# A hybrid decoder block on one core: the input stage reordered, two sums of x as adding DMAs, rotation tables later

## The chip, the core and the metric

The kernel runs on one core of a Trainium2 chip. The metric is device time in microseconds (us) of one execution; lower is better. All times of the trace are microseconds from the start of the profiled span.

## The reference

One layer, 1024 tokens of width 1024, float32:

```python
h = rms_norm(x, mix_norm_g)
z_a, q, k, v, gate_logits = split(h @ w_in)                  # w_in: 1024 x 5888
y_a = chunked_spatial_gating(gelu(z_a), ...)                 # chunks of 128 tokens, 4 channel groups
y_b = dilated_mixture_attention(rope(q), rope(k), v)         # 3 groups of 4 heads of 64
merged = sigmoid(g_a) * (y_a @ w_branch_a) + sigmoid(g_b) * (y_b @ w_branch_b)
x = x + merged @ w_out
h2 = rms_norm(x, ffn_norm_g)
a, val = split(h2 @ w_up)                                    # 2 x 2816 columns
x = x + (gelu(causal_dwconv3(a)) * val) @ w_down
return rms_norm(x, final_norm_g)
```

The rotation `rope` turns the first 16 of 64 dimensions of each head by angles `position * inv_freq`. The change lies wholly in how `h @ w_in` begins.

## The kernel before

**Products in parts.** Every large product is made of float32 operands that are split in two: `hi`, rounded to the matmul's float32r format by ScalarE, and `lo`, the rest, a subtraction on VectorE. Three passes (hi x hi, hi x lo, lo x hi) give the product. A 128x512 operand thus costs one ScalarE and one VectorE instruction, and a product over half the width (QK = 4 tiles of 128) twelve matmuls of 128x512.

**The input product.** Its columns go in pairs of 2 x 128 columns (`PAIRS`): three pairs `zv`, then three pairs each for the attention groups, then gates and `zu`. x stands in `X` transposed (channels on the partitions): 8 rows `kt` of 1024 tokens. `quarter(i, j, kt)` is its block of tokens half `i` and channel half `j`: A11, A12 (i = 0), A21, A22 (i = 1).
- Pairs 0 and 1 are plain products (`plain_step`, `plain_final`): for pair n, token half h and column half i, 24 matmuls over all 8 rows, on parts of the *raw* x times the gain (`raw_left`). The norm's factor per token is applied later, when V is written out of PSUM (`turn_v`).
- From pair 2 (`FIRST`) on, each pair takes seven products P1 to P7 instead of eight (Strassen's scheme in Winograd's form). Their left operands (`LEFT`) are parts of the *scaled* x: A11, A12, A22 and the sums S1 = A21 + A22, S2 = S1 - A11, S3 = A11 - A21, S4 = A12 - S2; the right ones are columns of w_in and sums of them (`weight_op`). P2 goes on in P1's PSUM bank, P4 in P7's and P3 in P5's (`SHARED`), after ScalarE or VectorE has read the first product out of it.

**The norm.** ScalarE squares the rows of x (`square_row`, tokens on the partitions, loaded by `load_rows`), POOL takes the root (`root`), VectorE makes four diagonals of it (`diagonal`), and TensorE multiplies them by ones (`spread`), which gives the factor of each token along the free axis. With it VectorE scales `X` in place (`scale_x`). All that happens for each token half h.

**The rotation tables.** `rot_tables` gives a chain of small VectorE steps (`some(n)` does the next n), two sines on ScalarE, sixteen widening copies on ScalarE (`wide`) and four turns (`turns`: four transposes on TensorE and a copy back on ScalarE each), whose result is in `YC` and is first needed by the rotation of pair 3.

**Order.** `beginning()` writes the order of VectorE, ScalarE and TensorE by hand up to pair 2's first product; then a loop over `in_order` does one product per step `i` (`in_product`), with `in_ahead` preparing operators ahead and `meanwhile(i)` the left operands that are missing. Up to `ORDERED` = 6, the end of pair 2, ScalarE and VectorE keep the written order; later a scheduler orders them. Loads are issued by SP in the order written. At step 3 the pool of `X` is closed: the tile V lies on its memory, and the copies of turned pairs into V (`turn_v`, two small PSUM banks, `ps_tr`) wait until the last part of x has been read.

In `beginning()` before, the plain products come in the order (pair, token half) = (0,0), (1,0), (0,1), (1,1); A11, A12 and A22 are split during them; the sums S1 and S2 are made on VectorE, S3 and S4 on POOL; the turns stand between the last plain products. `meanwhile` splits S3 after P1, S1 after P2 and S4 after P7.

Of the kernel before, what the change touches and what calls it, by code (L numbers as in the profile page):

```python
# [16 lines left out]
ALU = mybir.AluOpType  # L17
# [76 lines left out]
def block_kernel(  # L94
# [60 lines left out]
    def f32(ap):  # L155
        return ap.bitcast(F32)
# [189 lines left out]
    in_load(0, 1)  # L346
    in_load(1, 0)
    load_rows(0)
    in_load(1, 1)
    load_x(1, range(KT))  # L350
# [27 lines left out]
    def diagonal(h):  # L378
        for b in range(4):
            dg = dgs[h][:, b * P : (b + 1) * P]  # L380
            nc.vector.tensor_scalar(dg, ident, rss[h][:, b : b + 1], None, ALU.mult)
# [10 lines left out]

    def in_left(name, kt, src):

        arena, row = IN_ROWS[name]
        t = left[name, kt] = two(arena, row + kt)
        return (
            lambda: nc.scalar.activation(t[:, 0], src, AF.Copy),
            lambda: nc.vector.tensor_tensor(t[:, 1], src, f32(t[:, 0]), ALU.subtract),
        )  # L400
# [16 lines left out]
    def parts_of(name, i, j):  # L417
        staggered((lambda: None, *in_left(name, kt, quarter(i, j, kt))) for kt in range(QK))

    U_ROWS = {(0, 0): (R, 0), (0, 1): (R, 8), (1, 0): (G1, 0), (1, 1): (R, 12)}
# [18 lines left out]
    def x_sum(n, kt):  # L441
        a11, a12, a21, a22 = (quarter(i, j, kt) for i in range(2) for j in range(2))
        if n == 1:
            nc.vector.tensor_tensor(a22, a21, a22, ALU.add)
        elif n == 2:
            nc.vector.tensor_tensor(a11, a22, a11, ALU.subtract)
        elif n == 3:
            nc.gpsimd.tensor_tensor(a21, a11, a21, ALU.subtract)
        else:
            nc.gpsimd.tensor_tensor(a12, a12, a11, ALU.subtract)  # L450
# [573 lines left out]
    def beginning():  # L1024

        chain, wide, turns = rot_tables(
            nc, lent, [[C[2][:, i, lower], C[2][:, i, upper]] for i in range(2)],
            acc_tile, ident, positions, YC,
# [18 lines left out]
        def product(n, h, i, k):  # L1047
            for kt in range(QK):
                plain_step(n, h, i, k, kt)
# [3 lines left out]
        for k in range(2):  # L1053
            weight(0, k, 0)
            for kt in range(k * QK, (k + 1) * QK):
                raw_parts(0, kt)
            product(0, 0, 0, k)
# [3 lines left out]
        some(4)  # L1061
        weight(1, 0, 0)
        weight(1, 1, 0)
        plain_final(0, 0, 0)
        for k in range(2):
            product(0, 0, 1, k)
        some(10)
# [4 lines left out]
        plain_final(0, 0, 1)  # L1072
        diagonal(0)
        for k in range(2):
            product(1, 0, 0, k)
        bc0 = spread(0)
        weight(1, 0, 1)
        weight(1, 1, 1)
        for kt in range(KT):
            raw_parts(1, kt)  # L1080
            scale_x(0, kt, bc0)
            some(1)
        plain_final(1, 0, 0)
        for b in range(4):
            square_row(1, b)
        root(1)
        for k in range(2):
            product(1, 0, 1, k)
        some(99)
        plain_final(1, 0, 1)  # L1090
        diagonal(1)
        product(0, 1, 0, 0)
        bc1 = spread(1)
        parts_of("A11", 0, 0)
        product(0, 1, 0, 1)
        parts_of("A12", 0, 1)
        for fn in wide:
            fn()
        for kt in range(KT):
            scale_x(1, kt, bc1)  # L1100
        plain_final(0, 1, 0)
        for k in range(2):
            product(0, 1, 1, k)
        plain_final(0, 1, 1)
        parts_of("A22", 1, 1)
        for kt in range(QK):
            x_sum(1, kt)
            x_sum(3, kt)
        in_ahead(0, 9, 2)
        turns[0]()  # L1110
        for k in range(2):
            product(1, 1, 0, k)
        turns[1]()
        plain_final(1, 1, 0)
        turns[2]()
        for k in range(2):
            product(1, 1, 1, k)
        turns[3]()
        plain_final(1, 1, 1)
        staggered(  # L1120
            (lambda kt=kt: x_sum(2, kt), *in_left("S2", kt, quarter(0, 0, kt)))
            for kt in range(QK)
        )
        for kt in range(QK):
            x_sum(4, kt)
# [21 lines left out]
    beginning()  # L1147
# [1137 lines left out]
```

## Time and profile before

| | |
|---|---|
| median of 3 runs | 1397.3 us (1396.05 to 1397.56) |
| the profiled execution's own time | 1395.51 us |
| its span | 1393.3 us |
| TensorE matmuls busy | 1367.7 us, 98% of the span, 6434 instructions |
| VectorE, ScalarE, POOL busy | 74%, 47%, 22% of the span |
| mean granted TensorE clock | 0.994 |

The profile has a page and views that answer from the same trace. In a row of the timeline stand start, duration, engine, line of the kernel, operation, output and inputs, and the count of merged instructions; in brackets the idle time before it and what ended it. Rows of waits give waiter, releaser, total time, count and longest. PE is TensorE, PEld its weight loads, DVE VectorE, ACT ScalarE, POOL GpSimd, SP the engine that issues most DMAs.

### The profile page before, as it was taken

To read this page: it belongs to the slowest core of one execution; us is meant where nothing else is said; L and a number is where in the kernel's file an instruction comes from. 1 tells how busy PE (TensorE), PEld (TensorE's weight loads), DVE (VectorE), ACT (ScalarE), POOL (GpSimd) and SP (SyncE) were. 2 spreads that over 40 slices of the span, in tenths; PEclk is the share of its full clock that TensorE was granted. 3 is DMA by queue.
4 is the path that set the end of the run, shared out by engine and by line. 5 is a ranking of instruction groups with operands and counts; after the bars stand their busy time and mean duration, and the time that the engine had idled before them with its cause. 6 is when DMAs were issued, how large, how long until landed. Compare 5 with 4: busy or idle time off the path is not lost.

```text
span 1393.3 us, 19245 instructions
## 1 busy us (share of the span) xinstructions
PE 1367.7 (98%) x6434; PEld 1133.6 (81%) x6434; DVE 1036.0 (74%) x1884; ACT 653.7 (47%) x1285; POOL 306.7 (22%) x299
## 2 busy tenths in 40 slices
PE   9789999999999999999999999999999999999997
PEld 7667888888888888888888878888888888888886
DVE  7878677676876987867789887766766667685674
ACT  8473255555553432534546444433333335455453
POOL 1302000000232000030001046555566553000002
PEclk9999999999999999999999999999999999999999
DMA  9014635364435997594743133333333327996563
GB/s 362 18 50 123 180 97 181 96 178 129 139 111 168 330 318 271 187 310 168 266 137 119 39 113 106 106 106 104 104 105 119 121 83 245 385 317 229 196 207 121
DMA packets 142787, 234.91 MB, mean 169 GB/s; under 512 B 13664, under 2 KB 57440, under 8 KB 142688
## 3 DMA queue, kind: packets, MB, share of 16 engines
q1 hardware_dynamic: 141248, 231.53, 49.7%
q10 hardware_dynamic: 1440, 2.16, 0.4%
q8 instruction: 51, 0.84, 0.3%
q14 instruction: 48, 0.39, 0.1%
HBM read 167.77 MB, written 64.29 MB: 167 GB/s over the span
## 4 chain that ended last, share of the span: by engine, by line
PE 83%; DVE 6%; DMA 5%; issue 3%; ACT 1%; POOL 1%; POOLq 0%; DVEq 0%; SPq 0%; ACTq 0%
PE in_P L486 25%; PE uP L1762 19%; PE dn L2020 10%; PE up L1762 8%; PE pa L1234 5%; PE wo_P L1595 4%; PE pu L827 2%; DMA dS<-gS 2%; PE pu L1741 2%; PE pb L1234 2%; PE pl L547 1%; PE pp L811 1%; DMA X<-in_xt_dram 1%; PE sc L772 1%; PE sc L773 1%
## 5 line engine op out<-in xcount | busy, mean ns | idle before, releaser
L486 PE MATMUL in_P<-R,G 128*128 128x512 f32 x1008 | 247.4, 398 | 6.1 <-ACT C L506 4.4
L486 PEld LDWEIGHTS in_P<-R,G 128*128 128x128 f32 x1008 | 187.5, 190 | 44.5 <-ACT C L506 4.8
L2020 PE MATMUL dn<-R 128*128 128x512 f32 x924 | 209.6, 389 | 0.0
L2020 PEld LDWEIGHTS dn<-R 128*128 128x128 f32 x924 | 173.4, 188 | 36.0
L165 ACT ACTIVATE G<-wr 128x512 fp32r<-128x512 f32 x126 | 79.1, 629 | 152.0 <-PE in_P L486 111.6
L165 ACT ACTIVATE R<-up 128x512 fp32r<-128x512 f32 x130 | 78.7, 627 | 123.7 <-DVE up L278 40.9
L1762 PE MATMUL up<-G,R 128*128 128x512 f32 x504 | 121.5, 391 | 1.5 <-DVE R L166 1.5
L486 PE MATMUL in_P<-G,G 128*128 128x512 f32 x504 | 122.8, 393 | 0.2 <-DVE C L513 0.2
L1762 PE MATMUL uP<-G,R 128*128 128x512 f32 x504 | 121.2, 389 | 0.0
L1762 PE MATMUL uP<-R 128*128 128x512 f32 x504 | 121.1, 389 | 0.0
L1762 PEld LDWEIGHTS up<-G,R 128*128 128x128 f32 x504 | 94.5, 188 | 22.5 <-DVE R L166 2.0
L1762 PEld LDWEIGHTS uP<-G,R 128*128 128x128 f32 x504 | 94.6, 188 | 19.8
L1762 PEld LDWEIGHTS uP<-R 128*128 128x128 f32 x504 | 94.6, 188 | 19.7
L486 PEld LDWEIGHTS in_P<-G,G 128*128 128x128 f32 x504 | 92.8, 188 | 18.8 <-issue 0.6
L166 DVE TENSOR_TENSOR G<-wr,G 128x512 fp32r<-128x512 f32 x126 | 90.0, 715 | 20.9 <-ACT G L165 20.7
L166 POOL TENSOR_TENSOR R<-up,R 128x512 fp32r<-128x512 f32 x55 | 83.8, 1523 | 74.1 <-ACT R L165 74.1
L165 ACT ACTIVATE R<-db 128x512 fp32r<-128x512 f32 x77 | 48.1, 626 | 57.9 <-PE dn L2020 48.0
L166 DVE TENSOR_TENSOR R<-up,R 128x512 fp32r<-128x512 f32 x75 | 62.8, 839 | 16.1 <-ACT R L165 15.9
L166 DVE TENSOR_TENSOR R<-db,R 128x512 fp32r<-128x512 f32 x77 | 53.6, 699 | 25.8 <-ACT R L165 25.7
L1234 PE MATMUL pa<-R,G 128*128 128x512 f32 x288 | 67.9, 389 | 0.0
L878 POOL TENSOR_TENSOR ld<-ld,w 128x256 f32<-128x256 f32 x16 | 11.2, 719 | 236.5 <-DVE w L866 236.5
L1234 PEld LDWEIGHTS pa<-R,G 128*128 128x128 f32 x288 | 54.1, 188 | 11.2
(273 smaller groups left out, 2462.1 us busy)
## 6 DMA issues: line engine op xcount, KB each, us to landing
wr<-in_w_in_dram SPq DMA_DIRECT2D x45, 512.0 KB, 4.1
up<-in_w_up_dram SPq DMA_DIRECT2D x44, 512.0 KB, 3.5
dA<-gd SPq DMA_DIRECT2D x55, 256.0 KB, 4.8
wd<-in_w_down_dram SPq DMA_DIRECT2D x44, 256.0 KB, 5.3
wT<-wd SPq DMA_DIRECT2D x44, 256.0 KB, 3.9
dS<-gS SPq DMA_DIRECT2D x44, 256.0 KB, 4.3
db<-wT SPq DMA_DIRECT2D x44, 256.0 KB, 4.3
gd<-Y SPq DMA_DIRECT2D x42, 256.0 KB, 2.0
```

What stands on the lines that cost most here:

```text
L165: nc.scalar.activation(hi, src, AF.Copy)
L166: fn = lambda: lo_eng.tensor_tensor(lo, src, f32(hi), ALU.subtract)
L486: nc.tensor.matmul(acc, op[:, w, kt, :], left[LEFT[name], kt][:, a, :], start=opened and kt == 0 and i == 0, stop=kt == QK - 1 and i == 2, ...
L547: nc.tensor.matmul(acc, plain_ops[n, k, i][:, w, kt, :], raw_x[h, k * QK + kt][:, a, :], start=k == 0 and kt == 0 and p == 0, stop=k == 1 ...
L772: nc.tensor.matmul(dst, self.qa[:, h, :], keys, start=True, stop=False)
L773: nc.tensor.matmul(dst, self.qb[:, h, :], keys, start=False, stop=True)
L827: nc.tensor.matmul(pu[:, h * HD : (h + 1) * HD], self.pT[:, i, :], vt[:, h * HD : (h + 1) * HD], start=i % n == 0, stop=i % n == n - 1,)
L1234: nc.tensor.matmul(acc, unit[a][kt // 4][:, kt % 4, :], two(R, 8 * h + kt)[:, b, :], start=n == 0 and i == 0, stop=n == len(kts) - 1 and i ...
L1595: nc.tensor.matmul(acc, left[LEFT[name], kt][:, a, blk * P : (blk + 1) * P], out_ops[s][:, w, :], start=name not in SHARED and kt == 0 and ...
L1741: nc.tensor.matmul(acc, plain_up[which, k][:, w, kt, :], left[f"A{h + 1}{k + 1}", kt][:, a, :], start=n == 0 and i == 0, stop=n == KT - 1 ...
L1762: nc.tensor.matmul(acc, op[:, w, kt, :], left[LEFT[name], kt][:, a, :], start=opened and kt == 0 and i == 0, stop=kt == QK - 1 and i == 2, ...
L2020: nc.tensor.matmul(accs[blk], dops[s][:, 0, a, blk * P : (blk + 1) * P], dops[s][:, 1, w, :], start=SEQ[j] not in CONTINUES and kt == 0 an ...
```

## The change

- **Loads.** The right half of x (tokens 512 to 1023) is loaded before pair 1's weights and the rows for the squares, not after them.
- **Order of the plain products.** Pair 0 for both token halves, then pair 1: (0,0), (0,1), (1,0), (1,1). So the raw right half is split (`raw_parts(1, kt)`) straight after pair 0's first products, and the second squares come after pair 0's last product.
- **Signs.** The first diagonal is negated, so the left half of `X` holds -A11 and -A12; A11, A12, S3 and S4 are split with the sign turned (`NEGATED`). The second diagonal is made by ScalarE.
- **Sums.** S1 goes into `Z`, a view of `YC`, beside the scaling of the right half (VectorE); S2 = Z + (-A11) is on VectorE; -S3 and -S4 are made in place by DMAs that add into their destination, issued by POOL, four of 512 KB (`x_sum_dma`).
- **Parts.** A22, split during the plain products before, is split at step 2 of the loop, S4 again at step 3. S2 is split during the last plain products.
- **Rotation tables.** The end of the chain and the widening stand at step `ORDERED`, after pair 2, the turns two steps later; the widened tables lie in `YC`, the turns take the two small PSUM banks (`tr_tile`) instead of the large ones.

```diff
     in_load(0, 1)
+    load_x(1, range(KT))
     in_load(1, 0)
     load_rows(0)
     in_load(1, 1)
-    load_x(1, range(KT))
...
         for b in range(4):
-            dg = dgs[h][:, b * P : (b + 1) * P]
-            nc.vector.tensor_scalar(dg, ident, rss[h][:, b : b + 1], None, ALU.mult)
+            dg, rs = dgs[h][:, b * P : (b + 1) * P], rss[h][:, b : b + 1]
+            if h == 0:
+                nc.vector.tensor_scalar(dg, ident, rs, -1.0, ALU.mult, ALU.mult)
+            else:
+                nc.scalar.activation(dg, ident, AF.Copy, scale=rs)
...
+    NEGATED = ("A11", "A12", "S3", "S4")
...
+        if name in NEGATED:
+            return (
+                lambda: nc.scalar.activation(t[:, 0], src, AF.Copy, scale=-1.0),
+                lambda: nc.vector.scalar_tensor_tensor(
+                    t[:, 1], src, -1.0, f32(t[:, 0]), ALU.mult, ALU.subtract
+                ),
+            )
...
+    Z = YC.rearrange("p i (a t) -> p (i a) t", a=2)
...
     def x_sum(n, kt):
...
         if n == 1:
-            nc.vector.tensor_tensor(a22, a21, a22, ALU.add)
-        elif n == 2:
-            nc.vector.tensor_tensor(a11, a22, a11, ALU.subtract)
-        elif n == 3:
-            nc.gpsimd.tensor_tensor(a21, a11, a21, ALU.subtract)
+            nc.vector.tensor_tensor(Z[:, kt], a21, a22, ALU.add)
         else:
-            nc.gpsimd.tensor_tensor(a12, a12, a11, ALU.subtract)
+            nc.vector.tensor_tensor(a11, a11, Z[:, kt], ALU.add)
+
+    def x_sum_dma(n, k):
+
+        def q(i, j):
+            kt = j * QK + 2 * k
+            return X[:, kt : kt + 2, (lower, upper)[i]]
+
+        dst, src = {3: (q(1, 0), q(0, 0)), 4: (q(0, 1), q(0, 0))}[n]
+        nc.gpsimd.dma_start(dst, src, accum_op=ALU.add)
...
     def meanwhile(i):
         if i == 0:
-            parts_of("S3", 1, 0)
+            parts_of("S3")
         elif i == 1:
-            parts_of("S1", 1, 1)
+            parts_of("S1")
+        elif i == 2:
+            parts_of("A22")
         elif i == 3:
-            parts_of("S4", 0, 1)
+            parts_of("S4")
...
+        elif i == ORDERED:
+            some(99)
+            for fn in wide:
+                fn()
+        elif i == ORDERED + 2:
+            for fn in turns:
+                fn()
```

The new order of `beginning()`, from the second product on:

```python
        plain_final(0, 0, 0)
        product(0, 0, 1)
        for kt in range(KT):
            raw_parts(1, kt)
        product(0, 1, 0)
        plain_final(0, 0, 1)
        weight(1, 0, 0)
        weight(1, 1, 0)
        for b in range(4):
            square_row(0, b)
        load_rows(1)
        root(0)
        some(14)
        diagonal(0)
        plain_final(0, 1, 0)
        weight(1, 0, 1)
        weight(1, 1, 1)
        product(0, 1, 1, (0,))
        for kt in range(QK):
            plain_step(0, 1, 1, 1, kt)
            if kt == 2:
                bc0 = spread(0)
        for kt in range(KT):
            scale_x(0, kt, bc0)
        plain_final(0, 1, 1)
        for b in range(4):
            square_row(1, b)
        root(1)
        parts_of("A11")
        product(1, 0, 0)
        diagonal(1)
        bc1 = spread(1)
        for kt in range(QK):
            scale_x(1, kt, bc1)
            scale_x(1, kt + QK, bc1)
            x_sum(1, kt)
            if kt % 2 == 1:
                x_sum_dma(3, kt // 2)
        plain_final(1, 0, 0)
        product(1, 0, 1)
        plain_final(1, 0, 1)
        parts_of("A12")
        in_ahead(0, 9, 2)
        product(1, 1, 0)
        plain_final(1, 1, 0)
        for kt in range(2):
            x_sum(2, kt)
        parts_of("S2", range(2))
        product(1, 1, 1)
        in_ahead(0, 9, 3)
        for kt in range(2, QK):
            x_sum(2, kt)
        parts_of("S2", range(2, QK))
        plain_final(1, 1, 1)
        for k in range(2):
            x_sum_dma(4, k)
```

More of the change, by code (lines that the diff above doesn't have):

```diff
@@ L1026, in beginning @@
         chain, wide, turns = rot_tables(
-            nc, lent, [[C[2][:, i, lower], C[2][:, i, upper]] for i in range(2)],
-            acc_tile, ident, positions, YC,
+            nc, lent, [[YC[:, i, lower], YC[:, i, upper]] for i in range(2)],
+            tr_tile, ident, positions, YC,
         )
@@ L1086, in beginning @@
         root(1)
[L1087 to L1125 removed]
+        parts_of("A11")
+        product(1, 0, 0)
+        diagonal(1)
+        bc1 = spread(1)
+        for kt in range(QK):
+            scale_x(1, kt, bc1)
+            scale_x(1, kt + QK, bc1)
+            x_sum(1, kt)
+            if kt % 2 == 1:
+                x_sum_dma(3, kt // 2)
+        plain_final(1, 0, 0)
+        product(1, 0, 1)
+        plain_final(1, 0, 1)
+        parts_of("A12")
+        in_ahead(0, 9, 2)
+        product(1, 1, 0)
+        plain_final(1, 1, 0)
+        for kt in range(2):
[6 more added lines that the diff above has]
+        parts_of("S2", range(2, QK))
+        plain_final(1, 1, 1)
+        for k in range(2):
+            x_sum_dma(4, k)
+        return some, wide, turns
     def meanwhile(i):
         if i == 0:
[L1129 removed]
+            parts_of("S3")
         elif i == 1:
[L1131 removed]
+            parts_of("S1")
+        elif i == 2:
+            parts_of("A22")
         elif i == 3:
[L1133 removed]
+            parts_of("S4")
             x_stack.close()
@@ L1146, in block_kernel @@
     )
-    beginning()
+    some, wide, turns = beginning()
     for i, (n, name) in enumerate(in_order):
```

40 lines of the change are left out of this document (20 added, 20 removed).

## The prediction

> **What bounds the kernel now.** The page first:
>
> ```profile
> span 1393.3 us, 19245 instructions
> PE 1367.7 (98%) x6434; PEld 1133.6 (81%) x6434; DVE 1036.0 (74%) x1884; ACT 653.7 (47%) x1285; POOL 306.7 (22%) x299
> ```
>
> TensorE is busy for 98% of the span, and the change gives it the same products and transposes. It can pay only where TensorE stood still or ran slowly. The waits of TensorE, longest first, say where it stood:
>
> ```profile
> PE rs_bc L387 <- DVE C L381: 5.7, 1, 5.7
> PE in_P L486 <- ACT C L506: 4.4, 1, 4.4
> PE in_P L486 <- ACT G L165: 1.7, 1, 1.7
> ...
> PE up L1762 <- DVE R L166: 1.5, 1, 1.5
> ...
> PE vt L599 <- ACT V L604: 0.6, 1, 0.6
> ```
>
> All but the 1.5, which comes far behind, lie in the first 91 us, the stage that is rewritten. The stage by windows (us, busy time and count of PE, PEld, DVE, ACT, POOL, then granted clock, DMA share, GB/s) shows what follows such a stop:
>
> ```profile
> 42.00:44.00 2.00, 2.00 (x6) 1.55 (x6) 2.00 (x4) 2.00 (x5) 0.00 (x0) 0.50 0.00 0
> ...
> 72.00:74.00 2.00, 2.00 (x6) 1.55 (x5) 2.00 (x4) 1.28 (x3) 0.00 (x0) 0.50 0.00 0
> ...
> 80.00:82.00 2.00, 2.00 (x7) 1.54 (x6) 1.04 (x2) 2.00 (x5) 0.00 (x0) 0.56 0.00 0
> ```
>
> The clock is halved after each of the three stops, even after the one of 1.7 us. TensorE's rows of the timeline give the prices:
>
> ```profile
> 11.29 13.96 PE L547 MATMUL pl<-R,G 128*128 128x512 f32 x59 [0.19 <-DVE R L432]
> ...
> 40.02 2.08 PE L387 MATMUL rs_bc<-C,ones 128*128 128x128 f32 x8 [5.68 <-DVE C L381]
> 41.75 4.14 PE L547 MATMUL pl<-R,G 128*128 128x512 f32 x12
> 45.73 2.88 PE L547 MATMUL pl<-G 128*128 128x512 f32 x12
> 48.45 2.88 PE L547 MATMUL pl<-R,G 128*128 128x512 f32 x12
> ...
> 71.25 4.61 PE L486 MATMUL in_P<-R,G 128*128 128x512 f32 x12 [4.42 <-ACT C L506]
> 77.51 7.61 PE L486 MATMUL in_P<-R,G 128*128 128x512 f32 x24 [1.65 <-ACT G L165]
> ...
> 90.70 0.66 PE L599 MATMUL vt<-ident,C 128*128 128x128 f32 x4 [0.57 <-ACT V L604]
> ...
> 96.31 1.27 PE L599 MATMUL vt<-ident,C 128*128 128x128 f32 x8
> ...
> 103.71 7.08 PE L486 MATMUL in_P<-R,G 128*128 128x512 f32 x30
> ```
>
> Twelve matmuls start 2.72 apart when warm (45.73 to 48.45), 0.227 each; 3.98 when cold (41.75 to 45.73). The first stop thus costs 1.3 there, and 1.0 more in the spread, whose eight passes take 2.08 at half the clock. 4.61 against 2.88 is 1.7 lost behind the second stop, 7.61 against 5.6 (2.88 + 2.72) 2.0 behind the third. Stops (12.4) and slow stretches (6.0) together cost about 18 us. How much of this goes is the question.
>
> **The change, part by part.** ScalarE and VectorE work in a written order, so I follow the three queues with the intervals of these rows:
>
> ```profile
> 6.37 2.54 ACT L431 ACTIVATE R<-X,chan 128x512 fp32r<-128x512 f32 x4
> ...
> 21.03 1.03 POOL L374 TENSOR_TENSOR rs_x<-me_x,mhalf 128x4 f32<-128x4 f32 x1
> ...
> 22.10 0.87 DVE L381 TENSOR_SCALAR C<-ident,rs_x 128x128 f32<-128x128 f32 x4 [2.21 <-POOL rs_x L374]
> ...
> 27.98 1.06 ACT L366 ACTIVATE C<-C 128x1024 f32<-128x1024 f32 x1
> ...
> 29.26 1.06 ACT L366 ACTIVATE C<-C 128x1024 f32<-128x1024 f32 x1
> ...
> 40.44 4.26 ACT L398 ACTIVATE R<-X 128x512 fp32r<-128x512 f32 x8
> 41.09 4.91 DVE L399 TENSOR_TENSOR R<-X,R 128x512 fp32r<-128x512 f32 x8 [0.54 <-ACT R L398]
> ...
> 44.60 3.28 ACT L2212 ACTIVATE C<-ones 128x128 f32<-128x128 f32 x16
> ...
> 45.92 5.35 DVE L439 SCALAR_TENSOR_TENSOR X<-X,chan,rs_bc 128x512 f32<-128x512 f32 x8
> ...
> 74.67 0.68 DVE L276 TENSOR_TENSOR wt<-wr 128x512 f32<-128x512 f32 x1
> 75.38 0.69 DVE L277 TENSOR_TENSOR wr<-wr,wr 128x512 f32<-128x512 f32 x1
> ```
>
> And from the chain that ended last, in order of time, two pieces of the input's transfers:
>
> ```profile
> 9.30 8.91 DMA YC<-in_x_dram
> 18.23 7.10 DMA X<-in_xt_dram
> ```
>
> From start to start: squares 1.28; ScalarE high parts 0.52 (4.26 less the last 0.6, over 7), 0.61 with a gain; narrow copies 0.205; VectorE low parts 0.605, with a scalar 0.66; dependent sums 0.71.
>
> *To the first scale.* By 18.23 the queue had moved 5.5 MB, in the next 7.10 another 2.5 MB. With the order turned, the right half of x (5 MB) is in by about 17 and the rows by 18.2 + 5.7 = 23.9. ScalarE splits the right half from 14.9 to 19.8 (8 x 0.61). TensorE asks for it after its 48th matmul: the first 72 ended at 25.1, so at 25.1 - 24 x 0.227 = 19.6. No wait. Squares from 21.4 end at 26.4 (3 x 1.28 + 1.15), root and diagonal take 2.3 (20.7 to 22.97): 28.7. TensorE wants them at 25.1 + 21 x 0.227 = 29.9, so this scale stays hidden by 1.2. The four plain products of pair 0 end at 31.4 (with 0.8 for the spread).
>
> *The second scale.* Its squares stand behind the eviction of that last product: 32.2, end 37.2. Then four A11 parts (2.1), during which POOL does the root, and the diagonal, now on ScalarE: 4 x 0.29 (0.205 plus the 0.09 that a pointer scale adds), 39.2 to 40.4. TensorE has done pair 1's first product at 31.4 + 5.45 = 36.8 and stands 2.8; the spread ends at 41.0. So the 5.7 shrinks, it does not go. A slow stretch follows, at 1.7 as behind the second stop before. The three plain products left (3 x 5.45) then end at 59.0.
>
> *VectorE's chain from there.* Scaling and two-row sums: 8 x 0.66 + 4 x 0.605 and dependences, 8.2, to 49.2. A12 (4 x 0.66), operators P1 and P2 (53.1), two sums, two S2 parts, the first waiting for its high part: 55.8. Three dependent sums, and operator P6, which must pass ScalarE (0.63): 59.2. Two sums and two S2 parts: 61.9. S3 (its high parts follow the copy of P1, 62.4) and two operators: 66.7. ScalarE's table load (1.28), P2's eviction (0.6) and a high part come before S1: 67.9; S1, 70.3; operator P4 through ScalarE, 72.3; P6's sum, A22 (formerly split during the plain products), operator P3, P7's sum: 76.5; S4: 79.1. Uncontended intervals are used because POOL's eight sums are gone:
>
> ```profile
> 54.94 4.68 DVE L444 TENSOR_TENSOR X<-X 128x512 f32<-128x512 f32 x4
> ...
> 55.70 6.77 POOL L448 TENSOR_TENSOR X<-X 128x512 f32<-128x512 f32 x4 [20.86 <-DVE X L444]
> ```
>
> ```profile
> swap<-C SPq DMA_DIRECT2D x6, 256.0 KB, 3.6
> ```
>
> Beside POOL (first fence), VectorE's sums took 1.2 instead of 0.6. The four adding DMAs of 512 KB have no row; the nearest among the DMA issues is the move inside SBUF (second fence), 256 KB in 3.6. From below 3.6, from above twice 7.2 for adding and size, 14; I take 5, near the row, since it is also a move inside SBUF and no other transfer runs then. The first is issued at about 45.2 and its readers, VectorE's sums with all behind them, come at 53.1: 7.9 of cover; the second has 10, the last two over 13. I cost them at nothing. The Trainium skill, DMA: Bandwidth & Descriptors, Anatomy of one DMA, fits 2.0 us plus bytes over 436 GB/s, an estimate of 3.2 here, which leaves the sum as it is; no run here shows it.
>
> *TensorE through pair 2.* P1 follows at 59.0, ends at 61.7; P2 goes on in its bank and waits for the copy, which stands behind the last S2 part on ScalarE, to 62.4: 0.7 for the old 4.4. P2, P6, P7, P5 with two transposes end at 74.1. P4 shares P7's bank and waits for P7's sum, 76.5: a new stop of 2.4. The transposes after P4's first half (78.0) need a bank whose eviction into V waits, as before, for S4's last part, because V lies over x:
>
> ```profile
> 89.81 1.57 ACT L604 ACTIVATE V<-vt,rs_x 128x256 f32<-128x256 f32 x4 [1.90 <-DVE G L399]
> ```
>
> Behind 79.1 that is 80.0: another 2.0. Before, these transposes ran at 90.70, so the lead is 10.7. To P3's end (96.31) it took 5.6. Two stops with 1.4 of work between them halve the clock again; ScalarE's evictions hide a little: 1.3. Lead 9.4.
>
> *The rotation tables.* Their last 17 small VectorE steps now follow P3's last sum, mixed with five wide ones:
>
> ```profile
> L2167 DVE TENSOR_TENSOR ones<-ones 128x128 f32<-128x128 f32 x13 | 3.7, 288 | 0.2
> ...
> L2230 ACT ACTIVATE YC<-rot 128x512 f32<-128x512 f32 x4 | 2.4, 596 | 7.0 <-PE rot L2229 7.0
> ```
>
> With P3's end as zero: the sum ends at 1.1 (0.3 to its start, as at the other sums, and its own time), 17 x 0.245 (the widest kind has 288 ns) and 5 x 0.61 bring 8.3; two sines and an eviction of V that stands between, 9.3; sixteen widenings at 0.205, 12.7. TensorE comes at 8.8 (96.31 to 103.71 + 6 x 0.227 = 105.07). The first two turns need four and eight widenings (10.2, 11.1). The other two need the two small banks back, whose evictions stand behind all sixteen: 13.3 and 13.9, done at 14.2. Formerly the turns had the larger pool and no wait. That is 5.4 on the path, turns included (about 1.5, spared earlier and already in the lead), plus 1.4 of slow clock: 6.8.
>
> Sum: 9.4 - 6.8 = 2.6 us gained. After 105 no wait is over 1.5, and ScalarE and VectorE are delayed no more than TensorE. The profiled execution took 1395.51 (span plus 2.2), giving 1392.9; the median of the runs is 1.8 higher, giving 1394.7. A measurement here can tell about 0.2%, 2.8 us, so the forecast lies at that mark.
>
> **Rivals.** *No slow stretches.* If stops of 2 to 2.8 us leave the clock whole, P3 ends 1.3 and the turns 1.4 earlier; the stretch behind the second scale is hidden by VectorE anyway. The gain is 5.3: 1392.0. Against it stands the 1.65 us stop with 0.56 behind it; for it, that this stop followed a half-idle stretch. The Trainium skill, TensorE: Matmul & The Clock Gate, Part 1, says that it takes an idle window of about 3.4 us, which is this rival; the 0.56 disagrees.
>
> *The adding DMAs are late.* Each us beyond 7.9 for the first delays VectorE's sums, the whole chain and V's evictions one for one. At 10.5 the gain is gone, from 13.3 the kernel is slower by over 0.2%; at the upper end, 14, it takes 1394.7 + 6.1 = 1400.8. For it: no row shows such a DMA. Against it: idle DMA queues (share 0.00 in the window at 42), and the 3.6.
>
> *The stops only move.* Two slow stretches behind the turns and behind V's evictions instead of one each (1.7 more twice, less what ScalarE hides) leave -0.8 to 0: 1397.7. The rows at 40 to 44 show such a double stretch, after 5.7 us of rest.
>
> **Chances.** Forecast 0.58, split at the mark (0.26 faster, 0.32 same); clock kept 0.20; DMA late 0.08; stops only moved 0.14 (0.10 same, 0.04 slower). So faster 0.46, same 0.42, slower 0.12. The forecast's own range is 2.0 either way, for the intervals of a chain of 38 us: 1392.7 to 1396.7. The whole range takes in the clock rival with the same 2.0 (1390.0) and, above, the moved stops with 0.8 more (1398.5); the late DMA and the rest, under 0.2, stay outside.
>
> **What would show it.** In the profile after: a wait at the spread near 37 of 2 to 4 us; P2's wait under 1.5; P4 waiting for P7's sum and transposes for V, 4 us together; the turns at 96 to 103 with 3 to 4 us of waits on ScalarE. Wrong would be no wait at the turns, a wait of VectorE's sums on the adding DMAs, or clocks near 1.0 behind the stops.

## The result, and the profile after

| | before | changed |
|---|---|---|
| median | 1397.43 us (4 runs, 1396.05 to 1398.39) | 1390.32 us (4 runs, 1388.23 to 1391.52) |
| ratio, 95% interval | | 0.9948 (0.9931 to 0.9966) |
| the profiled execution's own time, its span | 1395.51, 1393.3 us | 1391.06, 1389.1 us |

The changed kernel is 0.52% faster: 7.1 us by the medians (4.8 to 9.6 by the interval), 4.5 us between the two profiled executions. Two later series gave 0.9957 (0.9942 to 0.9972) and 0.9966 (0.9953 to 0.9978), so the gain is about 5 to 7 us, where 2.6 was forecast. The page and the waits of TensorE after:

```profile
span 1389.1 us, 19247 instructions
PE 1364.6 (98%) x6434; PEld 1130.7 (81%) x6434; DVE 1030.6 (74%) x1880; ACT 655.1 (47%) x1289; POOL 298.1 (21%) x295
```

```profile
PE in_P L510 <- DVE C L537: 2.3, 1, 2.3
PE in_P L510 <- ACT C L530: 1.8, 1, 1.8
PE rs_bc L391 <- ACT C L385: 1.8, 1, 1.8
PE up L1788 <- DVE R L166: 1.7, 1, 1.7
...
PE rot L2255 <- ACT YC L2256: 1.4, 1, 1.4
...
PE vt L623 <- ACT V L628: 1.3, 1, 1.3
PE rot L2255 <- ACT YC L2238: 1.1, 1, 1.1
```

The 5.7, 4.4 and 1.7 of before became 1.8 at the spread (L391), 1.8 at P2 (for the copy of P1, L530), 2.3 at P4 (for P7's sum, L537), 1.3 at the transposes for V (L623) and 1.4 + 1.1 at the turns (L2255): the five places that the prediction named. TensorE's timeline after:

```profile
38.49 1.37 PE L391 MATMUL rs_bc<-C,ones 128*128 128x128 f32 x8 [1.75 <-ACT C L385]
39.62 5.73 PE L571 MATMUL pl<-R,G 128*128 128x512 f32 x24
...
60.71 8.48 PE L510 MATMUL in_P<-R,G 128*128 128x512 f32 x36 [1.76 <-ACT C L530]
...
75.14 1.96 PE L510 MATMUL in_P<-G,G 128*128 128x512 f32 x6 [2.33 <-DVE C L537]
78.38 1.12 PE L623 MATMUL vt<-ident,C 128*128 128x128 f32 x4 [1.28 <-ACT V L628]
79.15 2.91 PE L510 MATMUL in_P<-G,G 128*128 128x512 f32 x6
...
96.03 1.45 PE L2255 MATMUL rot<-ident,YC 128*128 128x128 f32 x8 [1.13 <-ACT YC L2238]
98.90 1.14 PE L2255 MATMUL rot<-ident,YC 128*128 128x128 f32 x8 [1.42 <-ACT YC L2256]
99.80 5.73 PE L510 MATMUL in_P<-R,G 128*128 128x512 f32 x24
```

Behind the spread and behind the turns 24 matmuls take 5.73: full clock. Behind the stops of P4 and of V's transposes six take 2.91 instead of 1.64: half clock. The product P2 of pair 3 starts at 99.80; before it began with the 7th of the 30 matmuls at 103.71, at 105.07. The lead there is 5.27 us. At the span's end it is 4.2: between 400 and 1000 us TensorE idles 3.5 us (before 2.9), where the rest goes was not followed up.

### The profile page after: what moved, and what is told of

Same layout as the page of the kernel before. It is cut to its first block, busy times and chain, and to the rows that moved or that the text cites. A ratio compares the mean times of both kernels' runs of the same rounds, so it can differ in the third digit from the quotient of the medians.

```text
span 1389.1 us, 19247 instructions
## 1 busy us (share of the span) xinstructions
PE 1364.6 (98%) x6434; PEld 1130.7 (81%) x6434; DVE 1030.6 (74%) x1880; ACT 655.1 (47%) x1289; POOL 298.1 (21%) x295
## 4 chain that ended last, share of the span: by engine, by line
PE 85%; DVE 6%; ACT 3%; issue 2%; POOL 2%; DMA 2%; SPq 0%; POOLq 0%; ACTq 0%; DVEq 0%
PE in_P L510 25%; PE uP L1788 19%; PE dn L2046 13%; PE up L1788 8%; PE pa L1260 5%; PE wo_P L1621 4%; PE pl L571 2%; PE pu L1767 2%; PE pb L1260 1%; PE pu L851 1%; DMA ld<-scr 1%; PE pp L835 1%; DVE G L166 1%; PE pm L660 1%; POOL st L903 1%
## 5 line engine op out<-in xcount | busy, mean ns | idle before, releaser
L510 PE MATMUL in_P<-R,G 128*128 128x512 f32 x1008 | 243.8, 394 | 1.8 <-ACT C L530 1.8
L1788 PEld LDWEIGHTS uP<-R 128*128 128x128 f32 x504 | 94.6, 188 | 19.6
L510 PE MATMUL in_P<-G 128*128 128x512 f32 x252 | 62.2, 393 | 0.0
```

The lines of the kernel that those rows point to most:

```text
L510: nc.tensor.matmul(acc, op[:, w, kt, :], left[LEFT[name], kt][:, a, :], start=opened and kt == 0 and i == 0, stop=kt == QK - 1 and i == 2, ...
L1788: nc.tensor.matmul(acc, op[:, w, kt, :], left[LEFT[name], kt][:, a, :], start=opened and kt == 0 and i == 0, stop=kt == QK - 1 and i == 2, ...
```

## The experiments

All medians stand beside the kernel before on the same chip; ratios with their intervals are to that.

**The changed kernel again** (nothing edited), in two series.

> The changed kernel once more, nothing altered, to see how far its executions scatter. Its trace showed TensorE 5.3 us ahead at the end of the rotation turns and 4.2 at the span's end, the medians 7.1. Theory A (the clock's stretches of 3.41 us run on by themselves, so the same stop leaves the clock whole in one execution and halves it in the next): the scatter stays 2 to 4 us, the gain lies between 4 and 7.5 us, and a second trace shows the same four stops with the same lengths to 0.3 us, but a slow stretch in another place or of another length than the 6.8 us from 76.3 to 83.1. Theory B (the slow stretch belongs to the stop at the fourth product of the pair): it stands in the same place with the same 6.8 us.

> The changed kernel beside the two that follow, on their chip, as their base. Expected: a gain over before of 5 to 7 us, as in the first two series, with the four stops at the same places. In its trace, by theory A (free-running stretches of 3.41 us, halved clock behind one with less than about 48% of full work), slow stretches stand where the phase puts them: behind the spread only if under 1.6 us of work lies in the stretch with the stop.

Measured: 1391.29 (1388.3 to 1394.58) against 1397.13, ratio 0.9957; and 1391.06 (1390.4 to 1394.23) against 1396.38, ratio 0.9966: 5.3 us by the medians, 4.7 by the ratio. In the three traces of this kernel the waits at the spread (1.75), at P4 (2.31 to 2.33) and at the turns (1.13 to 1.15 and 1.42) repeat. The slow stretches do not. In the first trace of the changed kernel there was one, 76.2 to 83.1; in the second one behind the spread too (38.8 to 42.2); in the third one from 75.4 to 82.2. Theory A holds: with the same order of instructions the half clock stands elsewhere, or once more. Two stops change with it: P2's is 0.74 in the second trace, since the slow stretch behind the spread has eaten the idleness there, and 1.76 in the third; V's is 1.28, 1.15 and 0.67. A fourth trace of this order (the first try of the late DMAs, below) has half clock for 3.4 us only, and there the turns start at 93.82 instead of 96.03, 96.22 and 95.53. So the lead of 5.27 above belongs to one execution.

**The second diagonal on VectorE.**

```
-                nc.scalar.activation(dg, ident, AF.Copy, scale=rs)
+                nc.vector.tensor_scalar(dg, ident, rs, None, ALU.mult)
```

> The second diagonal is built on VectorE, as in the kernel before, and stands there behind the four low parts of A11. The stop of TensorE at the second spread should grow from 1.75 to about 2.6 us (diagonal from 39.1 instead of 38.05). Theory A (prediction's: a stop of 2 to 2.8 us halves the clock behind it): the 24 matmuls behind the spread take 7 us or more instead of 5.73, and the kernel loses 0.9 to 2.5 us against the changed one. Theory B (clock judged by stretches of 3.41 us at least about half idle): the stop may lie across two stretches; then 5.73 and a loss of 0.9 us or less, since the stop at P1's copy and the one at P7's sum can take it up. If the vector chain alone sets the pace, the loss is 0.9 in full.

```profile
38.94 1.16 PE L391 MATMUL rs_bc<-C,ones 128*128 128x128 f32 x8 [2.63 <-DVE C L385]
39.85 7.31 PE L571 MATMUL pl<-R,G 128*128 128x512 f32 x24
```

The stop is 2.63 and the 24 matmuls take 7.31, so a stop of this length does halve the clock. Yet the kernel takes 1392.09, 0.8 more than the changed one in this series, with intervals that overlap (0.9965, 0.9952 to 0.9977), so no loss is shown. P2's wait falls to 0.75 and takes most of it up.

**Work in the stops.** Matmuls of the identity, unread, ahead of P4; then, in a second run, also ahead of the second spread, with the turns later (below).

```
+        elif i == 4:
+            fill = acc_tile("fill")
+            for _ in range(8):
+                nc.tensor.matmul(fill[:, :P], ident, ident, start=True, stop=True)
```

In the second run, besides:

```
         diagonal(1)
+        fill = acc_tile("fill1")
+        for _ in range(6):
+            nc.tensor.matmul(fill[:, :P], ident, ident, start=True, stop=True)
         bc1 = spread(1)
...
-        elif i == ORDERED + 2:
+        elif i == ORDERED + 4:
```

> Eight small matmuls of the identity, whose result nobody reads, stand ahead of the fourth product of the first pair (P4), in the stop of 2.3 us that waits for P7's sum. They take about 2.1 us there, so no product is delayed. Theory A (the stop's idleness halves the clock): the slow stretch from 76.3 to 83.1 us goes or shrinks, P3 of this pair ends 1.5 to 2.5 us earlier, and the kernel gains as much. Theory B (VectorE and the evictions into V set the pace of these products, the clock only fills their waits): clock 1.00 there, but the stop at the V transposes grows by as much, and the gain is under 0.7 us.

> The changed kernel with the turns two products later and unread small matmuls in two stops: six ahead of the second spread (1.6 of 1.75 us), eight ahead of P4 (2.1 of 2.3 us). Theory A (the clock falls behind a stretch of 3.41 us with less than about 48% of full work, so two filled stops leave it whole): granted clock 1.00 from 20 to 125 us; against the kernel with the turns later alone (1387.6) it gains 1.5 to 2.5 us at P4, and nothing at the spread, because the stop at the copy of P1 grows from 0.8 to about 1.8 there. So 1385 to 1386. Theory B (the chains of VectorE and ScalarE set the pace): clock 1.00 and no gain over 0.7 us.

The stage from 72 to 86 us by windows (columns as in the prediction), first of the changed kernel, then with P4's stop filled, then with both filled:

```profile
72.00:86.00 14.00, 10.39 (x42) 7.95 (x41) 10.65 (x17) 9.42 (x21) 0.00 (x0) 0.76 0.31 97
```

```profile
72.00:86.00 14.00, 11.79 (x70) 9.47 (x69) 12.01 (x21) 10.66 (x25) 0.00 (x0) 1.00 0.32 99
```

```profile
72.00:86.00 14.00, 11.82 (x71) 9.48 (x70) 12.02 (x22) 10.67 (x25) 0.00 (x0) 1.00 0.31 93
```

The granted clock goes from 0.76 to 1.00. With P4's stop filled the turns start at 94.36 instead of 96.22 (the changed kernel in the same series): 1.9 us, as theory A had it. V's transposes came no earlier (78.60 against 78.64, their wait grew from 1.15 to 1.62); the 1.9 was won behind them. But behind the turns a slow stretch came in that execution (97.7 to 101.1) and took part of it; the median, 1389.88 (0.9947, 0.9934 to 0.9960), is not told apart from the changed kernel's. With both stops filled and the turns later the clock is 1.00 from 20 to 125 us: 1385.40 (0.9922, 0.9909 to 0.9936), the lowest median of all. By the ratios that is 1.4 us better than the turns later alone, a little under the 1.5 to 2.5 expected, and the two intervals overlap, so this gain is not shown by the times; that the time itself fell between 1385 and 1386 owes something to the series, in which before ran 1.5 us faster. The fill at the spread bought nothing there: P2's wait is 1.76 again. The six executions lie within 1.7 us (1384.42 to 1386.11), those of the changed kernel within 3.3 to 6.3 in its three series.

**The turns two products later.**

```
-        elif i == ORDERED + 2:
+        elif i == ORDERED + 4:
```

> The sixteen transposes of the rotation tables stand two products later (behind P7 of the next pair instead of behind P6). Theory A (prediction's step: they cost 5.4 us on the path of which 3 to 4 are waits for the widenings and the two small banks): their waits on ScalarE (1.1, 0.4, 1.4) go, the turns take 1.8 to 2.2 us, and the kernel gains 2.5 to 3.5 us against the changed one. Theory B (ScalarE has the same work anyway, and the evictions and operators queued behind it are late next): the wait moves to a product's operator or to the transposes of the spatial stage, and the gain is under 1 us.

1387.63 (0.9932, 0.9919 to 0.9945), 3.7 us less than the changed kernel in this series. Of the three waits at the turns one of 0.85 is left:

```profile
100.13 1.03 PE L2255 MATMUL rot<-ident,YC 128*128 128x128 f32 x8
102.02 1.14 PE L2255 MATMUL rot<-ident,YC 128*128 128x128 f32 x8 [0.85 <-ACT YC L2256]
```

Theory A, a little beyond its 2.5 to 3.5: the turns' waits lay on the path, and the prediction's price for them (5.4 with the turns themselves) was right; 5.17 passed in the changed kernel between P6's end (93.27 + 6 x 0.227 = 94.63) and 99.80.

**The four adding DMAs as sums on POOL.**

```
-        nc.gpsimd.dma_start(dst, src, accum_op=ALU.add)
+        for j in range(2):
+            nc.gpsimd.tensor_tensor(dst[:, j], dst[:, j], src[:, j], ALU.add)
```

> The four adding DMAs become eight sums on POOL, at the same places. In the kernel before, four such sums took 6.77 us, and VectorE's sums beside them 1.17 instead of 0.64 us. Theory A (prediction's: the adding DMAs are hidden and cost nothing, and taking the sums from POOL spares VectorE that contention): VectorE's chain grows by 1.5 to 4 us (scaling and low parts beside POOL slower), the stop at P7's sum grows, and the kernel loses 1 to 3.5 us against the changed one (1391.3 in this series: 1392.3 to 1394.8). Theory B (it does not matter who adds, since the sums are needed late): the same time within 0.7 us.

1393.76 against 1395.59 (0.9987, 0.9977 to 0.9996). The changed kernel's ratios were 0.9948 to 0.9966, so 3 to 5 us of its gain are gone: theory A, at the upper end of its range or beyond. With the sums on POOL the rest of the change gains 0.13% (0.04 to 0.23). VectorE, POOL and TensorE of this kernel:

```profile
53.77 3.30 DVE L412 TENSOR_TENSOR R<-X,R 128x512 fp32r<-128x512 f32 x2
```

```profile
53.21 3.31 POOL L475 TENSOR_TENSOR X<-X 128x512 f32<-128x512 f32 x2 [3.70 <-DVE X L465]
```

```profile
63.40 10.55 PE L511 MATMUL in_P<-R,G 128*128 128x512 f32 x36 [4.86 <-ACT C L531]
```

Beside POOL's sums two low parts of S2 take 3.30; in the changed kernel, 1.29:

```profile
53.08 1.29 DVE L412 TENSOR_TENSOR R<-X,R 128x512 fp32r<-128x512 f32 x2
```

It happens twice, and A12's low parts lose another 1.1; P2's wait grows from 1.76 to 4.86. The Trainium skill, SBUF — State Buffer, section "SBUF: two separate sides", says that a VectorE instruction with two inputs in SBUF and a GpSimd instruction that reads SBUF compete for a shared pair of ports, which the one that starts first holds for its whole length. The trace agrees for these subtractions: 1.65 each on both engines, where VectorE's took 0.65 and POOL's sums beside the scaling 1.30, and the ends of the four alternate (POOL 54.82, VectorE 55.37, POOL 56.52, VectorE 57.07). The scaling of x, whose second operand is in PSUM, kept its time beside POOL's sums (1.40 for two).

**The adding DMAs late.** A first try moved both DMAs behind all scaling in the text alone:

```
-            if kt % 2 == 1:
-                x_sum_dma(3, kt // 2)
+        for k in range(2):
+            x_sum_dma(3, k)
```

> The first two adding DMAs are issued together behind all scaling, instead of one in its middle: the first about 4 to 6 us later (44.4 to about 48.5 or 50.4 us), the second about 1.3 us behind it. Theory A (prediction's rival: what the DMA is late beyond its cover delays VectorE's whole chain one for one; in the changed kernel the first lands at about 50.1, its reader starts at 51.7, so 1.6 us are spare): VectorE's first S2 sum waits 2 to 4 us, and the kernel loses 1.5 to 4 us against the changed one. Theory B (the sums are needed late and other stops take it up): the sum waits, and the loss is under 0.7 us.

The scheduler gave POOL the same order as before the edit, and the first DMA was issued at 44.08: this run is one more execution of the changed kernel's order (1390.85, 0.9965) and says nothing of late DMAs. The second try swapped them and held POOL to the written order too.

```
-        for k in range(2):
+        for k in (1, 0):
             x_sum_dma(3, k)
...
-        tc.manual_schedule(engines={mybir.EngineType.DVE, mybir.EngineType.Activation})
+        tc.manual_schedule(
+            engines={mybir.EngineType.DVE, mybir.EngineType.Activation, mybir.EngineType.Pool}
+        )
```

> The first two adding DMAs change places in POOL's queue: the one over the last rows, which waits for all scaling and sums of two rows (done at about 48.2 us), goes first, the one over the first rows second. In the changed kernel the four were issued at 44.4, 50.4, 55.7 and 61.1, each about when the one before it had landed (5.0 to 5.7 us from issue). Theory A (they run one at a time, and what is late beyond the cover delays VectorE's chain one for one, as the rival of the late DMAs has it): issues at 48.2 to 48.5 and 53.4 to 54, the second lands near 59, VectorE's first S2 sum waits for it from 51.7 to about 59, 7 us, the stop at the copy of P1 grows from 1.8 to about 8 us, and the kernel loses 6 to 9 us against the changed one: 1397 to 1400. Theory B (two may run side by side): the second is issued right behind the first, at about 49.5, and lands by 55: a wait of 3 us and a loss of 2 to 4. Theory C (other stops take it up): under 1 us.

POOL in the changed kernel, then POOL, VectorE and TensorE with the DMAs swapped:

```profile
44.40 1.42 POOL L474 DMA_DIRECT2D X<-X  x1 [6.94 <-DVE YC L463]
50.39 1.24 POOL L474 DMA_DIRECT2D X<-X  x1 [4.58 <-DVE R L406]
55.73 1.21 POOL L474 DMA_DIRECT2D X<-X  x1 [4.09 <-DVE wr L277]
61.05 1.22 POOL L474 DMA_DIRECT2D X<-X  x1 [4.12 <-DMA X<-X]
```

```profile
48.26 1.42 POOL L474 DMA_DIRECT2D X<-X  x1 [11.02 <-DVE YC L463]
53.76 1.24 POOL L474 DMA_DIRECT2D X<-X  x1 [4.08 <-issue]
```

```profile
58.85 1.29 DVE L465 TENSOR_TENSOR X<-X,YC 128x512 f32<-128x512 f32 x2 [7.30 <-DMA X<-X]
```

```profile
67.87 10.56 PE L510 MATMUL in_P<-R,G 128*128 128x512 f32 x36 [9.16 <-ACT C L530]
```

Theory A: the second issue stands 5.5 behind the first, though it waits for no other engine ("issue"), VectorE waits 7.30 and TensorE 9.16. V's transposes start at 86.30 instead of 78.38, 7.9 later. 1399.15 against 1396.39 (1.0025, 1.0014 to 1.0036): slower than before, about 8 us above the changed kernel by the medians and 8 to 11 by the ratios, where 6 to 9 was expected. The held order of POOL was not run without the swap, but the wait on the DMA stands in the trace itself. The rival of the late DMAs had the mechanism and the exchange rate right; its condition just did not occur.

**Only the tables later, in the kernel before.** Widened in YC and turned in the small banks.

```
-            some(1)
...
-        some(99)
...
-        for fn in wide:
-            fn()
...
-        turns[0]()
...
+        elif i == ORDERED:
+            some(99)
+            for fn in wide:
+                fn()
+        elif i == ORDERED + 2:
+            for fn in turns:
+                fn()
```

> The kernel before with one part of the change alone: the rotation tables' last steps, widenings and turns behind the first pair, in the small banks, everything else as before. Theory A (prediction's split): the stop at the second spread (5.7 us) waits for VectorE, where 16 table steps stand before the diagonal; without them it shrinks by about 4 us to 1.5 to 2, and ScalarE loses 3.3 us of widenings; the late turns take back 4 to 5.4 us. Net against before (1397.1): 0 to 1.5 us faster, so most of the change's gain comes from the new order of raw halves, squares and sums. Theory B (the tables are the change's whole gain): 4 us or more faster, near 1392.

```profile
35.84 1.16 PE L387 MATMUL rs_bc<-C,ones 128*128 128x128 f32 x8 [2.09 <-DVE C L381]
65.06 4.56 PE L486 MATMUL in_P<-R,G 128*128 128x512 f32 x12 [6.26 <-ACT C L506]
```

The spread's stop shrinks from 5.68 to 2.09 and the V transposes come 6.2 us earlier, but the late turns give nearly all of it back (P2 of pair 3 at 104.79 against 105.07), and the whole is 1399.39 against 1395.59: 0.18% slower (0.05 to 0.31). No gain comes from the tables alone; theory B falls, and theory A's 0 to 1.5 us was too kind. Of the 2.8 us that its profiled execution loses from there to the end, 0.5 is a slow stretch behind the turns (102.5 to 105.9) and 1.4 more idle time of TensorE between 400 and 1000 us (4.3 against 2.9); the rest was not followed up.

**Rearranged VectorE and ScalarE.** First A22 behind P7's sum and the V transposes two ticks later; then three idle times of VectorE filled by order. Both with the turns later, the second with the fill at the spread.

```
-        elif i == 2:
-            parts_of("A22")
         elif i == 3:
+            parts_of("A22")
             parts_of("S4")
...
-                after(1 + b // 2, lambda b=b: turn_v(1, C[1], b))
-                after(5 + b // 2, lambda b=b: turn_v(0, C[0], b))
+                after(3 + b // 2, lambda b=b: turn_v(1, C[1], b))
+                after(7 + b // 2, lambda b=b: turn_v(0, C[0], b))
```

> The turns two products later; A22 is split behind P7's sum instead of ahead of it, and the transposes for V stand two ticks (twelve matmuls) later. Theory A (two stops, 2.3 us for P7's sum and 1.1 for V's evictions, with the slow stretch of 6.8 us behind them, are all due to the written order): they go, and against the kernel with the turns later alone (1387.6) this gains 3.5 to 6 us: 1381.6 to 1384.1. Theory B (VectorE's chain to S4's last low part at 77.4 us bounds P3 anyway, and the evictions into V then pile up ahead of the widenings): the stops move to P3 and to the next pair's first copy, and the gain is under 1.5 us.

1394.75 (0.9995, 0.9984 to 1.0005): 7 us by the medians, 0.63% by the ratios, worse than the turns later alone. P4's stop fell to 0.85, but:

```profile
PE vt L623 <- ACT V L628: 6.6, 2, 4.7
...
PE in_P L510 <- DVE C L539: 1.8, 1, 1.8
```

Theory B: P3 now waits for P4's sum behind S4's low parts on VectorE, and the last V eviction stands behind the sines and sixteen widenings in ScalarE's written order; TensorE waits 4.75 for it.

The second run:

```
+        plain_final(1, 1, 1)
         for kt in range(2, QK):
             x_sum(2, kt)
         parts_of("S2", range(2, QK))
-        plain_final(1, 1, 1)
...
             parts_of("S3")
+            parts_of("S1")
         elif i == 1:
-            parts_of("S1")
-        elif i == 2:
             parts_of("A22")
```

> The turns two products later, six small matmuls in the spread's stop, and VectorE's three idle times before S4 filled by order: the last plain copy ahead of the second S2 half (0.5 us), S1's parts directly behind S3's, ahead of P2's copy and its table load (1.3), and A22's parts one product earlier (0.8, and no longer ahead of P7's sum). Theory A (VectorE's written order sets these stops): S4's last low part ends at about 75 instead of 77.4 us, P4's stop falls from 2.3 to under 0.7 and V's from 1.1 to 1.6 to under 0.9, the clock stays 1.00 there, and the kernel gains 3 to 5 us over the one with the turns later alone, which stood at 0.9932 of before: 0.9895 to 0.991. Theory B (operators and V's evictions on ScalarE, or the transposes, set the pace): under 1 us, or a loss.

1387.36 (0.9933, 0.9919 to 0.9946), no better than the turns later alone. VectorE's 0.80 and 1.32 before S4 shrank to 0.31 and 0, but 1.00 came up ahead of A22 (ScalarE's table load and P2's copy now stand before it), S4 began at 73.96 instead of 74.91, and P4 still waited 1.86, in a slow stretch:

```profile
73.36 0.68 DVE L537 TENSOR_TENSOR C<-C,in_P 128x512 f32<-128x512 f32 x1
```

```profile
74.19 1.99 PE L510 MATMUL in_P<-G,G 128*128 128x512 f32 x6 [1.86 <-ACT G L405]
```

The row names S4's high parts (L405), which P4 does not read. It shares P7's bank, and it starts 0.15 behind the end of P7's sum (74.04), just as in the changed kernel (74.99 and 75.14): the sum still sets this stop, and the new order brought it only 0.95 forward. Theory B.

## Why the prediction was right, and where its sizes were off

The time, 1390.32, lies on the forecast's side and in the whole range (1390.0 to 1398.5), 0.3 above its lower end. It lies outside the forecast's own range, 1392.7 to 1396.7: what took it in is the width that the rival "no slow stretches" lent, and that rival did not come true as it was put. So much is luck. The 7.1 us by the medians are also more than the traces can account for: the profiled execution of before stood 1.9 below its median, that of the changed kernel 0.7 above. By steps, in us from the span's start, of the changed kernel's first trace:

| step of the prediction | forecast | trace |
|---|---|---|
| right half of x asked for, no wait | 19.6 | 19.33, none |
| first diagonal, spread hidden | 28.7 | 28.35 to 29.23, none |
| squares of the second half done, ScalarE goes on | 37.2 | 35.97 |
| stop at the second spread | 2.8 | 1.75 |
| VectorE's scaling and sums end | 49.2 | 48.16 |
| P2's wait, its start | 0.7, 62.4 | 1.76, 60.71 |
| P4 starts, behind P7's sum | 76.5 (2.4) | 75.14 (2.33) |
| transposes for V | 80.0 (2.0) | 78.38 (1.28) |
| lead at the third V transpose, at P3's end | 10.7, 9.4 | 12.3, 10.2 |
| turns, on the path | 5.4 + 1.4 of slow clock | 5.17, no slow clock |
| lead at P2 of pair 3 | 2.6 | 5.27 |

The mechanism held at every place: the long stops shrink or move to where P7's sum, V's evictions and the late turns set them, and no wait of VectorE's sums on the adding DMAs appears. One of the signs of being wrong came in part: the clock was 1.00 behind the spread in three of the four traces of this order, and behind the turns in all four. And one margin was thinner than forecast: the rows for the first squares were in at 25.73 instead of 23.9, ScalarE waited 1.39 for the third, and the first diagonal ended 0.3 ahead of its spread (29.53) instead of 1.2. Three terms were mis-sized.

*The second squares* (0.8 of the 1.6 us by which V's transposes came early). I took 1.28 from start to start; after, it is 1.04:

```profile
31.81 1.05 ACT L366 ACTIVATE C<-C 128x1024 f32<-128x1024 f32 x1
...
32.85 1.05 ACT L366 ACTIVATE C<-C 128x1024 f32<-128x1024 f32 x1
```

The trace of before had this interval too, at the first two squares:

```profile
15.93 1.05 ACT L366 ACTIVATE C<-C 128x1024 f32<-128x1024 f32 x1
...
16.97 1.05 ACT L366 ACTIVATE C<-C 128x1024 f32<-128x1024 f32 x1
```

I had read the other row only, and its 1.28 is not ScalarE's pace but that of the loads: the four rows of x landed at 27.96, 29.23, 30.51 and 31.79, and each square started 0.02 to 0.03 behind its row. In the changed kernel every row is in before its square (the last at 32.91), so the four take 4.2 instead of 5.0. They also start 0.4 earlier, and VectorE needs 3.5 instead of 3.9 for A12 and the two operators behind the scaling. Together, squares, diagonal and spread, VectorE's whole chain and with it P7's sum and V's evictions came 1.0 to 1.7 earlier.

*The slow clock* (about 0.6). I charged a slow stretch behind the spread, 1.3 at V's stop and 1.4 at the turns. The one behind the spread came in one of the four traces of this order and costs little there, as the prediction's rival said (P2 starts at 60.96 with it, at 60.71 without). At V's stop it was longer than I thought: the lead falls by 2.1 instead of 1.3. At the turns none came in the four; with the second diagonal on VectorE, with P4's stop filled, and in the kernel before with the tables later, one did. So the rival "no slow stretches", which gives 1392.0, is nearest in time but not by its reason: stops of 1.75 to 2.6 us do halve the clock, only not always.

*The turns* (0.5): 5.17 instead of 5.4, from a point reached 0.3 earlier behind P3's end.

1.6 at V's transposes, -0.8 down to P3's end, and 1.9 at the turns (1.4 of clock, 0.5 of path) make the 2.7 by which 5.27 exceeds 2.6.

*The adding DMAs* were costed at nothing, rightly, but their cover was misread. The 5.0 to 5.7 us to landing in the changed kernel fit the 5 that I took. The estimate of 3.2 by the Trainium skill, DMA: Bandwidth & Descriptors, Anatomy of one DMA, falls short, and the measurement decides. But I gave the second one 10 us of cover as if it could start at once. They run one at a time, so its spare time is 57.73 - 50.39 - 5.1 = 2.2 us, and the first's 51.69 - 44.40 - 5.7 = 1.6. The swapped order shows what lies beyond.

Where the gain comes from: 3 to 5 us hang on POOL's sums being gone (theory A of the POOL run), and the tables alone gain nothing; the order of raw halves and squares was not tried by itself, so its share is not shown.

## What to carry to other kernels

A sum moved from GpSimd to an adding DMA also speeds up VectorE if GpSimd's sums ran beside it: look for VectorE's rows that are twice their usual length there. Cost such DMAs one after the other, and find for each the first reader and the first writer of what it reads. Where short stops remain on TensorE, moving work that waits for ScalarE behind more products gained (0.9932 of before), and with unread matmuls in the stops besides the clock stayed whole and the executions lay close together (0.9922, not told apart from 0.9932). The two new orders, tried on top of the later turns, moved the stops or shortened them a little and gained nothing (0.9995, 0.9933). Ask of a measured interval which engine set it before you price a step with it.

## What the runs showed of the hardware

TensorE's clock is judged by stretches of 3.41 us that run on by themselves: within each trace every change of clock lies a whole number of 3.41 us from every other. The Trainium skill, TensorE: Matmul & The Clock Gate, Part 1, has such a free-running window, and the traces agree. Its table has the half clock after one idle window; here much less idleness was enough. Stretches of the changed kernel, then of the same kernel again, then of the run with the DMAs' unchanged order:

```profile
35.28:38.69 3.41, 1.66 (x8) 1.08 (x7) 2.77 (x6) 3.41 (x9) 1.21 (x2) 1.00 0.51 209
38.69:42.10 3.41, 3.41 (x19) 2.98 (x19) 2.60 (x5) 1.11 (x4) 0.00 (x0) 1.00 0.00 0
72.83:76.24 3.41, 1.10 (x5) 0.96 (x6) 3.41 (x7) 2.43 (x5) 0.00 (x0) 1.00 0.38 108
76.24:79.65 3.41, 2.13 (x8) 1.38 (x7) 3.38 (x6) 2.08 (x5) 0.00 (x0) 0.50 0.31 119
```

```profile
35.34:38.76 3.42, 1.67 (x9) 1.13 (x8) 2.78 (x5) 3.42 (x10) 1.21 (x2) 1.00 0.29 117
38.76:42.17 3.41, 3.41 (x13) 2.93 (x13) 2.16 (x4) 0.85 (x3) 0.00 (x0) 0.50 0.00 0
```

```profile
71.42:74.83 3.41, 1.06 (x8) 0.72 (x6) 3.41 (x7) 3.41 (x7) 0.00 (x0) 1.00 0.51 154
74.83:78.25 3.42, 3.05 (x7) 1.95 (x8) 3.42 (x7) 1.19 (x4) 0.00 (x0) 0.50 0.50 153
78.25:81.66 3.41, 3.41 (x20) 2.83 (x19) 2.65 (x6) 2.30 (x7) 0.00 (x0) 1.00 0.16 46
```

A stretch at full clock in which TensorE was busy 1.10 of 3.41 us is followed by a half-clock one; 1.66 and 1.67, 49%, went both ways. At half clock, 2.13 busy leaves it halved for one more stretch, 3.05 releases it. Between 20 and 125 us of all fourteen traces, all 14 full-clock stretches up to 46% busy were followed by half clock, 6 of the 25 from 47 to 55%, and none from 57% on. So up to 1.45 us of rest in a stretch was safe in this stage, a stop of 1.7 to about 3 us depends on how the phase cuts it (an estimate from these shares), and the same order of instructions paid one, two or three stretches, each up to 1.7 us of work lost. The share is not the whole rule: far behind this stage, in the last of the rearranged runs, a stretch that was 66% busy (2.26 of 3.41 us from 423.42, sixteen of its matmuls only 64 columns wide) was followed by one at half clock, and no other run shows such a case.

Part of the scatter between executions goes with the clock. Of the 20 executions of the changed kernel's order, the two with a mean granted clock of 0.993 took 1394.2 and 1395.2 us, the eight with 0.995 or 0.996 1390.4 to 1394.6, and the ten with 0.997 to 0.999 1388.2 to 1391.5. About 4 us remain at nearly the same clock, and their cause is open.

The second finding is the queue of adding DMAs: 512 KB inside SBUF takes 5.0 to 5.7 us in the changed kernel (up to 6.8 in the edited ones), and GpSimd issues the next one 0.3 us behind the landing. In the changed kernel they landed at 50.13, 55.46 and 60.73, and the next issues stand at 50.39, 55.73 and 61.05. VectorE, which the rows name there, is not what held the second: what it reads was ready at 48.16. With the swap, where the second waits for nothing, the landing is at 53.49 and the issue at 53.76. Only the fourth waits for a DMA by the program itself ("<-DMA X<-X"). What holds the others back is not shown.
